# A fused trunk block: the first gain row spread by TensorE, indexer heads one projection later, and norm chains in a fixed queue order

## The chip, the cores and the metric

One Trainium2 chip, one core. The metric is the device time of one execution in microseconds (us); lower is better. The profile is one more execution, taken by the hardware profiler. In its rows PE is TensorE, PEld its weight loads, DVE is VectorE, ACT is ScalarE, POOL is GpSimd and SP is SyncE; a trailing q (SPq, POOLq) is that engine's own queue issuing a DMA.

## The reference, cut to what matters

```
def rms_norm(x, g):
    return x * rsqrt(mean(x*x) + 1e-6) * g

h = rms_norm(x, g_mix_pre)                      # x: 512 tokens x 1024
(lru_x, lru_gate, pool_in, q, k, v, q_idx, k_idx, w_idx, gates) = split(h @ w_in)
ya = rg_lru(conv(lru_x)) * gelu(lru_gate)       # recurrence branch
yb = multiscale_pool(pool_in)                   # pooling branch
score = sum_h w_idx[h] * relu(q_idx[h] @ k_idx) # 8 indexer heads, then top 128 keys
yc = attention(q, k, v over the chosen keys)    # sparse attention branch
merged = sum(sigmoid(gates) * (branch @ w_branch))
x = x + rms_norm(merged @ w_out, g_mix_post)
h = rms_norm(x, g_mem_pre)
x = x + rms_norm(cross_attention(h, mem) @ w_mem_o, g_mem_post)
h = rms_norm(x, g_ffn_pre)
x = x + rms_norm((silu(h @ w_gate) * (h @ w_up)) @ w_ffn_out, g_ffn_post)
```

All data are float32. The output is x, 512 x 1024.

## The kernel before, in words

**Precision.** Every float32 product is made of three TensorE products. An operand is split into a high part (ACT casts it, `A.copy`) and a low part (DVE or POOL subtracts, `V.tensor_sub`); `mm3` (lines 89 to 92) multiplies high by high, high by low and low by high into one PSUM bank. Each weight tile of 128 x 1024 is loaded by SP into one of six `raw` slots and split by `split_next` (lines 180 to 206). Activations with features on the partitions stand in `hh` and `hl`, 128 x 8 x 512.

**Order.** The program is traced by Python, and a planner then orders each engine's instructions by its own estimate of when they become ready; it takes what is earlier in the program first among those that are ready. Inside `tc.manual_schedule()` (the start, up to line 431) the traced order is kept. `tc.keep_in_program_order(ins)` keeps one instruction behind the one traced just before it on its engine; nothing else is held by it. All waits between engines are by semaphore, and each engine takes its own list strictly in order.

**Start.** SP loads the two halves of tokens 0 to 127, then the row `g_mix_pre` broadcast to all 128 partitions (512 KB written, `gain`, line 228), then tokens 128 to 255, two weight tiles, and the rest. TensorE multiplies the identity 15 times (`keep_warm`). For each of the four groups of 128 tokens: ACT squares and sums, `rstd` makes the root from a power on POOL and one Newton step on DVE, `start_norm` (line 317) multiplies by root and gain, `turn_pe` (line 294) transposes on TensorE, `turn_out` (lines 302 and 303) splits the result into `hh` and `hl`. The first products follow on tokens 0 to 255 (line 422).

**Indexer.** For each pair of heads m = 0 to 3 there is one projection (`unit`, 24 products of 512 columns). `stacked_queries` splits its result and sends it by four DMAs from SP into `QI`. `idx_heads(m)` makes six score products (line 451), each followed by a relu on ACT (line 459) and a multiply-add on DVE (lines 462 and 464). In the loop over m = 1 to 3, `idx_heads(m - 1)` follows the projection of pair m; `idx_heads(3)` follows the projection of keys and values. After it `value_task` transposes the values (line 516).

**Attention.** A written list of steps (line 797) sets in which tick each score (S), transposition (T) and value product (A) is traced.

**Norms between the sub-layers.** Class `Residual` holds one group of 128 tokens after a sub-layer: `scaled` (sum of squares on ACT, times gain on DVE, line 914), `scale` (root), `add` (to x, line 930), `square`, `scale2`, `norm` (line 939) and `turn` (transposition into `hh` and `hl`). After the cross attention's output projection, `project` calls `after_o(t)` when group t is complete. Groups 0 and 1 are turned within the projection. The FFN's first two column pairs (four weight tiles) are then multiplied for tokens 0 to 255; after the third tile stand `R[3].norm()` and the turn of group 2, after the fourth the turn of group 3. The tile products of tokens 256 to 511 follow.

**FFN.** From the third column pair on, a seven-product scheme (class `Pair`) works on sums of weight quarters and of token quarters. `token_sums` builds the token side; `first` to `fourth` build the weight side of the next pair while the current one is multiplied. `first` is line 1183's cast of a weight tile and line 1186's subtraction.

Of the kernel before, what the change touches and what calls it, by code (L numbers as in the profile page):

```python
# [9 lines left out]
F32 = mybir.dt.float32  # L10
F32R = mybir.dt.float32r
AF = mybir.ActivationFunctionType
OP = mybir.AluOpType
AX = mybir.AxisListType

P = 128
D = 1024
# [5 lines left out]
EPS = 1e-6  # L23
# [42 lines left out]
def hybrid_block_kernel(ctx: ExitStack, tc: tile.TileContext, a: dict, out: bass.AP):  # L66
    nc = tc.nc
    V, A, T, G, SP = nc.vector, nc.scalar, nc.tensor, nc.gpsimd, nc.sync

    base = ctx.enter_context(tc.tile_pool(name="base", bufs=1))  # L70
    psum = ctx.enter_context(tc.tile_pool(name="psum", bufs=1, space=bass.MemoryType.PSUM))
    PS = Slots(psum, "ps", 8, 512)
# [3 lines left out]
    GB = Slots(base, "gb", 2, 1024)  # L76
# [3 lines left out]
    T2 = Slots(base, "t2_", 10, 512)  # L80
# [5 lines left out]
    def f32(ap):  # L86
        return ap.bitcast(F32)
# [140 lines left out]
    def gain(name):  # L228
        g = GB.take([P, D])
        src = a[name]  # L230
        SP.dma_start(g, bass.AP(tensor=src.tensor, offset=src.offset, ap=[[0, P], [1, D]]))
        return g

    warm = base.tile([P, 1], F32, name="warm")
    V.memset(warm, 0.0)
    A.activation(warm, warm, AF.Tanh)
# [2 lines left out]
    V.memset(half, -0.5)  # L239
    for c in range(2):  # L240
        SP.dma_start(xs[0][:, 0, c * 512:(c + 1) * 512], x_in[0:P, c * 512:(c + 1) * 512])
    g_pre = gain("g_mix_pre")
    SP.dma_start(xs[0][:, 1], x_in[P:2 * P, :])
    load_ahead(2)
    SP.dma_start(xs[1][:, 0], x_in[2 * P:3 * P, :])
# [1 line left out]
    ident = base.tile([P, P], F32, name="ident")  # L247
# [8 lines left out]
    def keep_warm(n):  # L256

        ps = PS.take([P, P])
        for _ in range(n):
            T.matmul(ps, ident, ident, start=True, stop=True)  # L260
        PS.give(ps)

    start = tc.manual_schedule()
    start.__enter__()
    keep_warm(WARM[0])

    def rstd(parts):

        u, w, y, c = col(name="u"), col(name="w"), col(name="y"), col(name="c")
        if len(parts) > 1:  # L270
            V.tensor_scalar(u, parts[0], parts[1], EPS, op0=OP.add, op1=OP.add)  # L271
        else:
            V.tensor_scalar(u, parts[0], EPS, None, op0=OP.add)
        G.tensor_tensor(y, u, half, op=OP.pow)  # L274
        V.tensor_scalar(w, u, -0.5, None, op0=OP.mult)

        def finish():
            V.scalar_tensor_tensor(c, y, w, y, op0=OP.mult, op1=OP.mult)  # L278
            V.scalar_tensor_tensor(y, c, 1.5, y, op0=OP.add, op1=OP.mult)  # L279
            return y  # L280
        return finish

    def sum_sq(src, scratch):

        ss = col(name="ss")
        A.activation(scratch, src, AF.Square, scale=D ** -0.5, accum_out=ss)  # L286
        return ss

    def turn_pe(src):
# [8 lines left out]
    def turn_out(pss, hh, hl, t, last=True):  # L298
        dst = slice(t * P, (t + 1) * P)
        for q, ps in enumerate(pss):  # L300
            h = hh[:, 4 * q:4 * q + 4, dst]
            A.copy(h, ps)
            V.tensor_sub(hl[:, 4 * q:4 * q + 4, dst], ps, f32(h))  # L303
        if last:
            PS.give(*pss)

# [4 lines left out]
    hh, hl = HH.take([P, KD, S], F32R), HL.take([P, KD, S], F32R)  # L311
# [8 lines left out]
    ss = [sum_sq(*X0[1])]  # L320
# [4 lines left out]
    pss = turn_pe(X0[0][1])  # L325
# [5 lines left out]
    pss = turn_pe(X0[1][1])  # L331
# [6 lines left out]
    ss = [[sum_sq(*X0[t])] for t in range(2, 4)]  # L338
# [49 lines left out]
    def unit(o, w):  # L388
        unit_piece(o, w, 0, S)
        give_w(w)  # L390
# [90 lines left out]
    def idx_heads(m):  # L481
        for h in (2 * m, 2 * m + 1):
            for b in range(1, 4):
                idx_head(b, h)

    for m in range(1, 4):
        w = take_w()
        ps = PS.take([P, S])
        unit(ps, w)
        if m == 1:  # L490
            pw = PS.take([P, 4, 8])
            for t in range(4):
                T.transpose(pw[:, t], wf[64:72, t * P:(t + 1) * P], ident[64:72, 64:72])
            V.tensor_scalar(wq, pw, 8 ** -0.5, None, op0=OP.mult)
            PS.give(pw)
            T2.give(wf)
            vector_task()
            softplus_task()
        stacked_queries(ps, QI, m)
        PS.give(ps)  # L500
        idx_heads(m - 1)

    w = take_w()
    ps = PS.take([P, S])
# [3 lines left out]
    A.copy(vf[64:128], ps[64:128])  # L508
    PS.give(ps)

    idx_heads(3)

    def value_task():
# [16 lines left out]
    for i, name in enumerate(("lru_w_a", "lru_w_x")):  # L530
        t = T2.take([P, 4, P])
        G.memset(t, 0.0)
        src = a[name][0].rearrange("(m s) i j -> s i m j", s=2)
# [4 lines left out]
    t = T2.take([P, 4, P])  # L538
# [108 lines left out]
    for m in range(4):  # L647
        w = take_w()
        ps = PS.take([P, S])
# [5 lines left out]
    for g in GROUPS:  # L655
        w = take_w()
        ps = PS.take([P, S])
# [9 lines left out]
    for m in range(4):  # L667
        w = take_w()
        ps = PS.take([P, S])
# [123 lines left out]
    def steps_of(text):  # L793
# [1 line left out]
        return [(lambda s=s: kind[s[0]](int(s[1]), int(s[2]))) for s in text.split()]  # L795

    ticks = collections.deque(steps_of(t) for t in (
# [3 lines left out]

# [8 lines left out]
    for m in range(4):  # L810
        w = take_w()
        ps = PS.take([P, S])
# [58 lines left out]
    X = [xs[t // 2][:, t % 2] for t in range(4)]  # L871
# [36 lines left out]
    def scaled(pss, g, dst, scratch):  # L908

        ss = []  # L910
        for c in range(2):
            cs = slice(c * 512, (c + 1) * 512)
            ss.append(sum_sq(pss[c], scratch[:, cs]))
            V.tensor_mul(dst[:, cs], pss[c], g[:, cs])
        PS.give(*pss)
        return ss

    class Residual:
# [8 lines left out]
            self.f = rstd(self.ss)  # L927

        def add(self):
            V.scalar_tensor_tensor(X[self.t], self.b8[:, 0], self.f(), X[self.t], op0=OP.mult, op1=OP.add)  # L930

        def square(self):
            self.ss = [sum_sq(X[self.t], self.b8[:, 0])]
# [2 lines left out]
            self.f = rstd(self.ss)  # L936

        def norm(self):
            V.scalar_tensor_tensor(self.b8[:, 1], X[self.t], self.f(), self.g2, op0=OP.mult, op1=OP.mult)  # L939

        def turn(self, more=None):
            pss = turn_pe(self.b8[:, 1])
# [7 lines left out]
    hh, hl = HH.take([P, KD, S], F32R), HL.take([P, KD, S], F32R)  # L950
    R = []
# [20 lines left out]
    for m in range(4):  # L972
        w = take_w()
        ps = PS.take([P, NM])
# [19 lines left out]
    for i in range(4):  # L994
        w = take_w()
        for kk in range(2):
            k = 2 * i + kk
            for t in range(2):
                r = slice(t * P, (t + 1) * P)
# [63 lines left out]
    for h in range(4):  # L1063
        w = take_w()
        ps = PS.take([P, S])
# [21 lines left out]
    hh, hl = HH.take([P, KD, S], F32R), HL.take([P, KD, S], F32R)  # L1087
    R = []

    def after_o(t, pss):  # L1090
        R.append(Residual(t, pss, g_post, g_next))
        R[t].scale()
        R[t].add()
        R[t].square()
        R[t].scale2()
        if t < 3:
            R[t].norm()


    whole = K8.take([P, 2, 4, 256])  # L1100
# [14 lines left out]
    def last_heads():  # L1115
# [3 lines left out]
    project(lambda k: om[0][:, k], lambda k: om[1][:, k], 4, 4, after_o, [  # L1119
        (0, 0), lambda: mem_av(2), lambda: mem_tr(3), (0, 1), (0, 2), last_heads, (1, 0), (0, 3),  # L1120
        (1, 1), (1, 2), (1, 3), (2, 0), (2, 1), (2, 2), (2, 3), (3, 0), (3, 1), lambda: R[0].turn(turn_tokens),
        (3, 2), (3, 3), lambda: R[1].turn(turn_tokens)])
    K8.give(*om)


# [31 lines left out]
    def token_sums(t, c12, d1, d3):  # L1157

        r = slice((t - 2) * P, (t - 1) * P)
        d2, d4 = T2.take([P, 4, P]), T2.take([P, 4, P])  # L1160
        V.scalar_tensor_tensor(d2, d3, -1.0, whole[:, 0, :, r], op0=OP.mult, op1=OP.subtract)
        V.scalar_tensor_tensor(d4, d2, -1.0, whole[:, 1, :, r], op0=OP.mult, op1=OP.subtract)
        for name, src in (("t2", d2), ("t1", d1), ("t3", d3), ("t4", d4)):
            if name not in tokens:
                tile_ = K8.take([P, 2, 4, TH], F32R)
                tokens[name] = (tile_[:, 0], tile_[:, 1], tile_)
            h, l = (x[:, :, r] for x in tokens[name][:2])
            tc.keep_in_program_order(A.copy(h, src))
            tc.keep_in_program_order(V.tensor_sub(l, src, f32(h)))
        T2.give(c12, d1, d2, d3, d4)  # L1170
# [99 lines left out]
    pss = [PS.take([P, S]) for _ in range(NFIRST)]  # L1270
    for c in range(2):
        for i in range(NFIRST):
            unit_piece(pss[i], ws[i], c * 256, c * 256 + 256)
            if c == 0 and i == 2:
                R[3].norm()
                ds = R[2].turn(turn_tokens)
        if c == 0:
            token_sums(3, *R[3].turn(turn_tokens))
            token_sums(2, *ds)
            K8.give(whole)  # L1280
            tokens.update(b11=quad(0, 0), b21=quad(1, 0), b22=quad(1, 1))
            scratch = K8.take([P, 2, KD, P])
            cur = Pair(NFIRST // 2)
            for f in (cur.first, cur.sums, cur.second, cur.third, cur.fourth):
                f(f in (cur.first, cur.sums))
# [7 lines left out]
    old = None  # L1293
    while cur is not None:
        nxt = Pair(cur.m + 1) if cur.m + 1 < NFF else None
        if nxt is None:
            state["last"] = len(specs)
        cur.p1()
        if nxt:
            nxt.sums()  # L1300
        if old:
            old.p3()
        cur.p2()
        if old:
            old.p4()
        if nxt:
            nxt.first()
        cur.p6()
        if nxt:
            nxt.second()  # L1310
        cur.p5()
        cur.p7()
        if nxt:
            nxt.third()
            nxt.fourth()
        old, cur = cur, nxt
# [75 lines left out]
```

## Time and profile before

| | us |
|---|---|
| median of 3 runs | 889.28 (888.46 to 889.8) |
| the profiled execution | 890.12 |
| its span, first to last instruction | 888.3 |
| TensorE busy in the span | 867.3 (98%) |
| VectorE busy | 606.6 (68%) |
| ScalarE busy | 399.0 (45%) |
| GpSimd busy | 200.6 (23%) |

The profiled execution lies 0.84 us above the median of the runs. A busy share is the time in which an engine had an instruction running; a stretch in which TensorE has none is a wait, and the profile names what ended it. PEclk is the share of full clock that TensorE was granted: 1.00 is 2.4 GHz, 0.50 is 1.2 GHz.

### The profile page before, as it was taken

Reading aid. Unit: us, or ns where it says so; the run is one execution under the profiler, and the core shown is the slowest. Engines: PE = TensorE matmul, PEld = TensorE weight load, DVE = VectorE, ACT = ScalarE, POOL = GpSimd, SP = SyncE. Lnnn points to the kernel's source line nnn. Section 1 sums busy time; section 2 is a strip of 40 time slices with the busy share of each in tenths; the row PEclk is TensorE's granted clock in tenths of the full one; section 3 lists DMA queues with packets and bytes.
Section 4 is the critical chain, followed back from the end, with each engine's and each line's share of the span. In section 5 each row is a group of like instructions: output and inputs, shape, how many; then the busy total and the mean of one; then the engine's idle time right before and its main releaser. Section 6 shows DMA issues by size and latency. Waiting matters only on the chain. (4 is left out here: it accounts for less than half of the span.)

```text
span 888.3 us, 12970 instructions
## 1 busy us (share of the span) xinstructions
PE 867.3 (98%) x4923; PEld 754.6 (85%) x4923; DVE 606.6 (68%) x1089; ACT 399.0 (45%) x669; POOL 200.6 (23%) x195
## 2 busy tenths in 40 slices
PE   7999999999999999999999998999999999999996
PEld 7788888888878888888888878999999999888885
DVE  5859989973775656442696778987888878732225
ACT  4555644223654544331565554554554455522121
POOL 2223267454344423210110011111111110000000
PEclk8999999999999999999999999999999999999999
DMA  8953227333333237333265302677777775433102
GB/s 252 240 129 99 80 63 200 94 95 95 83 86 86 68 86 261 106 105 96 82 187 159 95 1 48 151 157 171 163 154 152 166 172 135 126 95 95 47 1 95
DMA packets 128570, 106.02 MB, mean 119 GB/s; under 512 B 6208, under 2 KB 112252, under 8 KB 128508
## 3 DMA queue, kind: packets, MB, share of 16 engines
q1 hardware_dynamic: 120172, 90.52, 36.0%
q0 software_dynamic: 5760, 10.49, 7.5%
q10 hardware_dynamic: 2576, 4.19, 1.4%
q8 instruction: 38, 0.62, 0.3%
q14 instruction: 24, 0.20, 0.1%
HBM read 86.83 MB, written 2.10 MB: 100 GB/s over the span
## 5 line engine op out<-in xcount | busy, mean ns | idle before, releaser
L191 ACT CAST wh<-raw 128x1024 fp32r<-128x1024 f32 (+1 forms) x104 | 108.6, 1047 | 228.3 <-PE ps L91 108.2
L90 PE MATMUL ps<-hh,wh 128*128 128x512 f32 (+2 forms) x584 | 207.2, 355 | 0.0
L91 PE MATMUL ps<-hl,wh 128*128 128x512 f32 (+2 forms) x584 | 206.3, 353 | 0.4 <-DVE hl L303 0.4
L92 PE MATMUL ps<-hh,wl 128*128 128x512 f32 (+2 forms) x584 | 206.3, 353 | 0.0
L195 DVE TENSOR_TENSOR wl<-raw,wh 128x1024 fp32r<-128x1024 f32 x60 | 73.8, 1235 | 102.7 <-ACT wh L191 102.7
L91 PEld LDWEIGHTS ps<-hl,wh 128*128 128x128 f32 (+1 forms) x584 | 109.3, 187 | 16.0 <-DVE hl L303 0.6
L90 PEld LDWEIGHTS ps<-hh,wh 128*128 128x128 f32 (+1 forms) x584 | 109.4, 187 | 15.9 <-ACT t L459 0.2
L92 PEld LDWEIGHTS ps<-hh,wl 128*128 128x128 f32 (+1 forms) x584 | 109.2, 187 | 15.9
L90 PE MATMUL ps<-k,wh 128*128 128x256 f32 (+1 forms) x368 | 114.6, 311 | 0.0
L92 PE MATMUL ps<-k,wl 128*128 128x256 f32 (+1 forms) x368 | 114.3, 310 | 0.0
L91 PE MATMUL ps<-k,wh 128*128 128x256 f32 (+1 forms) x336 | 105.3, 313 | 0.0
L198 POOL TENSOR_TENSOR wl<-raw,wh 128x512 fp32r<-128x512 f32 (+1 forms) x44 | 59.2, 1346 | 153.9 <-ACT wh L191 139.7
L274 POOL TENSOR_TENSOR y<-u,half 128x1 f32<-128x1 f32 x26 | 16.4, 631 | 304.8 <-DVE u L271 259.3
L92 PE MATMUL ps<-wh,k 128*128 128x512 f32 x192 | 75.8, 395 | 0.0
L92 PEld LDWEIGHTS ps<-k,wl 128*128 128x128 f32 x368 | 69.4, 188 | 4.3
L90 PEld LDWEIGHTS ps<-k,wh 128*128 128x128 f32 x368 | 69.3, 188 | 4.1
L91 PE MATMUL ps<-wl,k 128*128 128x512 f32 x176 | 69.4, 394 | 0.5 <-DVE wl L195 0.5
L1186 DVE TENSOR_TENSOR wl<-raw,wh 128x1024 fp32r<-128x1024 f32 x40 | 49.0, 1225 | 30.4 <-ACT wh L1183 30.1
L90 PE MATMUL ps<-wh,k 128*128 128x512 f32 x176 | 69.0, 394 | 0.0
L1183 ACT CAST wh<-raw 128x1024 fp32r<-128x1024 f32 x40 | 42.0, 1051 | 59.2 <-PE ps L91 52.9
L91 PEld LDWEIGHTS ps<-k,wh 128*128 128x128 f32 x336 | 63.3, 188 | 4.2
L199 POOL TENSOR_TENSOR wl<-raw,wh 128x512 fp32r<-128x512 f32 (+1 forms) x44 | 61.5, 1397 | 0.0
(250 smaller groups left out, 1697.7 us busy)
## 6 DMA issues: line engine op xcount, KB each, us to landing
raw<-in_w_in SPq DMA_DIRECT2D x45, 512.0 KB, 3.9
raw<-in_w_ffn_in SPq DMA_DIRECT2D x44, 512.0 KB, 4.8
raw<-in_w_ffn_out SPq DMA_DIRECT2D x22, 512.0 KB, 3.6
raw<-in_w_branch SPq DMA_DIRECT2D x12, 512.0 KB, 3.4
raw<-raw POOLq DMA_DIRECT2D x20, 256.0 KB, 3.7
raw<-k POOLq DMA_DIRECT2D x20, 256.0 KB, 3.3
k<-t SPq DMA_DIRECT2D x32, 128.0 KB, 2.4
raw<-in_w_out SPq DMA_DIRECT2D x8, 512.0 KB, 3.4
```

The lines of the kernel that those rows point to most:

```text
L90: T.matmul(o, lh, rh, start=start, stop=False, skip_group_check=True)
L91: T.matmul(o, lh, rl, start=False, stop=False, skip_group_check=True)
L92: T.matmul(o, ll, rh, start=False, stop=stop, skip_group_check=True)
L191: copy = A.copy(h, src)
L195: V.tensor_sub(l, src, f32(h))
L198: G.tensor_sub(l[:, :c], src[:, :c], f32(h[:, :c]))
L199: G.tensor_sub(l[:, c:], src[:, c:], f32(h[:, c:]))
L274: G.tensor_tensor(y, u, half, op=OP.pow)
L1183: copy = A.copy(h, src)
L1186: V.tensor_sub(l, src, f32(h))
```

## The change

Four edits. The gain row of the first norm is loaded once (4 KB, from ACT's queue, ahead of everything else there), turned on TensorE to a column and spread to all partitions by eight transpositions of broadcast columns, copied to SBUF by DVE; this stands ahead of `keep_warm`. The indexer heads of a pair follow one projection later. One tick of the attention list traces its scores ahead of its transposition. The chains of `Residual` after the cross attention are kept in traced order on ACT and DVE, with a new order for groups 0 and 1; the norm of group 3 moves into its chain; the turn of group 1 moves ahead of the projection's last block; the turns of groups 2 and 3 and the first cast of the fourth column pair are kept in order too.

```
+    grow = T2.take([8, P])
+    A.dma_start(grow, a["g_mix_pre"][0].rearrange("(k p) -> k p", p=P))
...
-    g_pre = gain("g_mix_pre")
...
     start = tc.manual_schedule()
     start.__enter__()
+    g_pre = GB.take([P, D])
+    gcol = base.tile([P, 8], F32, name="gcol")
+    ps = PS.take([P, 8])
+    T.transpose(ps, grow, ident[:8, :8])
+    V.tensor_copy(gcol, ps)
...
+    for q in range(2):
+        ps = PS.take([P, 4, P])
+        for k in range(4):
+            T.transpose(ps[:, k], gcol[:, 4 * q + k:4 * q + k + 1].to_broadcast([P, P]), ident)
+        V.tensor_copy(g_pre[:, q * 512:(q + 1) * 512], ps.rearrange("p k c -> p (k c)"))
+        PS.give(ps)
     keep_warm(WARM[0])
+    pins = {"on": False}
+    def queued(ins):
+        if pins["on"]:
+            tc.keep_in_program_order(ins)
...
-        idx_heads(m - 1)
+        if m > 1:
+            idx_heads(m - 2)
...
+    idx_heads(2)
     idx_heads(3)
...
-        "S00 S01", "S02 S03", "S10 S11", "T00 S12 S13",
+        "S00 S01", "S02 S03", "S10 S11", "S12 S13 T00",
...
     def after_o(t, pss):
+        pins["on"] = True
         R.append(Residual(t, pss, g_post, g_next))
+        if t == 1:
+            R[0].square()
         R[t].scale()
         R[t].add()
-        R[t].square()
-        R[t].scale2()
-        if t < 3:
-            R[t].norm()
+        for r in R[-2:] if t == 1 else R[t:] if t else ():
+            if r is not R[0]:
+                r.square()
+            r.scale2()
+            r.norm()
+        pins["on"] = False
...
-        (3, 2), (3, 3), lambda: R[1].turn(turn_tokens)])
+        (3, 2), lambda: R[1].turn(turn_tokens), (3, 3)])
...
             if c == 0 and i == 2:
-                R[3].norm()
+                pins["on"] = True
                 ds = R[2].turn(turn_tokens)
+                pins["on"] = False
         if c == 0:
-            token_sums(3, *R[3].turn(turn_tokens))
+            pins["on"] = True
+            ds3 = R[3].turn(turn_tokens)
+            pins["on"] = False
+            token_sums(3, *ds3)
...
-            nxt.first()
+            nxt.first(old is None)
```

The calls wrapped in `queued` are those of `rstd` on DVE, `sum_sq`, `turn_out`, the multiplication in `scaled`, `add` and `norm`.

## Rows read from the trace of the kernel before

**Rows 1.** The page's first part: busy us (share of span) xinstructions.

```profile
PE 867.3 (98%) x4923; PEld 754.6 (85%) x4923; DVE 606.6 (68%) x1089; ACT 399.0 (45%) x669; POOL 200.6 (23%) x195
```

**Rows 2.** Waits of TensorE, whole span: us in total, times, longest us.

```profile
PE ps L294 <- DVE k L317: 3.2, 2, 1.7
PE ps L294 <- DVE k L939: 3.1, 1, 3.1
PE ps L294 <- ACT wh L1183: 1.7, 1, 1.7
PE ps L451 <- DMA k<-t: 1.7, 1, 1.7
...
PE ps L516 <- ACT t L508: 0.7, 1, 0.7
PE ps L761 <- DVE t L751: 0.7, 1, 0.7
```

**Rows 3.** Timeline of the start, all engines: start us, us, instruction [idle before <-releaser].

```profile
1.42 6.12 PE L260 MATMUL ps<-ident 128*128 128x128 f32 x30 [1.42 <-POOL ident masks.py:199]
...
3.84 0.63 ACT L286 ACTIVATE k<-k 128x512 f32<-128x512 f32 x1 [1.60 <-DMA k<-in_x]
...
6.34 0.16 DVE L279 SCALAR_TENSOR_TENSOR y<-c,y 128x1 f32<-128x1 f32 x1
8.43 1.42 DVE L317 SCALAR_TENSOR_TENSOR k<-k,y,gb 128x512 f32<-128x512 f32 x2 [1.92 <-DMA gb<-in_g_mix_pre]
...
9.23 1.61 PE L294 MATMUL ps<-ident,k 128*128 128x128 f32 x8 [1.69 <-DVE k L317]
...
9.80 1.06 ACT L286 ACTIVATE k<-k 128x1024 f32<-128x1024 f32 x1 [4.63 <-DMA k<-in_x]
...
15.88 0.56 PE L90 MATMUL ps<-hh,wh 128*72 128x256 f32 x1
```

**Rows 4.** Windows of the start, PE alone: stretch, PE busy, PEclk, DMA share, GB/s.

```profile
10.00:17.00 7.00, 5.52 (x25) 0.51 1.07 318
```

**Rows 5.** Timeline of the indexer's heads: PE, then DVE.

```profile
39.28 1.29 PE L451 MATMUL ps<-ik,k 128*128 128x256 f32 x6 [1.68 <-DMA k<-t]
...
48.56 4.35 DVE L464 SCALAR_TENSOR_TENSOR sc<-t,wq,sc 128x256 f32<-128x256 f32 x6
```

**Rows 6.** Windows, all engines: PE, PEld, DVE, ACT, POOL busy (x), PEclk, DMA share, GB/s.

```profile
80.00:100.00 20.00, 20.00 (x89) 16.23 (x88) 20.00 (x41) 12.34 (x18) 2.54 (x3) 1.00 0.30 80
...
600.00:650.00 50.00, 50.00 (x426) 50.00 (x425) 41.14 (x62) 25.26 (x35) 8.66 (x10) 1.00 0.72 159
```

**Rows 7.** Timeline of the way from cross attention into the FFN: DVE and PE.

```profile
518.76 1.28 DVE L939 SCALAR_TENSOR_TENSOR k<-k,y,gb 128x1024 f32<-128x1024 f32 x1
...
526.12 1.28 DVE L939 SCALAR_TENSOR_TENSOR k<-k,y,gb 128x1024 f32<-128x1024 f32 x1
...
527.54 1.07 PE L294 MATMUL ps<-ident,k 128*128 128x128 f32 x8 [1.73 <-ACT wh L1183]
528.04 0.68 DVE L303 TENSOR_TENSOR hl<-ps,hh 128x512 fp32r<-128x512 f32 x1
...
535.00 1.28 DVE L939 SCALAR_TENSOR_TENSOR k<-k,y,gb 128x1024 f32<-128x1024 f32 x1
...
544.90 1.27 DVE L939 SCALAR_TENSOR_TENSOR k<-k,y,gb 128x1024 f32<-128x1024 f32 x1
...
546.32 1.94 PE L294 MATMUL ps<-ident,k 128*128 128x128 f32 x8 [3.09 <-DVE k L939]
...
561.17 1.22 DVE L1186 TENSOR_TENSOR wl<-k,wh 128x1024 fp32r<-128x1024 f32 x1
...
562.95 0.28 PE L90 MATMUL ps<-k,wh 128*128 128x256 f32 x1
```

**Rows 8.** Windows of the same way, PE alone: stretch, PE busy, PEclk, DMA share, GB/s.

```profile
528.50:532.50 4.00, 3.57 (x16) 0.57 0.02 4
546.00:550.00 4.00, 3.68 (x19) 0.57 0.18 33
```

More of the change, by code (lines that the diff above doesn't have):

```diff
@@ L264, in hybrid_block_kernel @@
     start.__enter__()
+    g_pre = GB.take([P, D])
[4 more added lines that the diff above has]
+    PS.give(ps)
+    T2.give(grow)
+    for q in range(2):
[3 more added lines that the diff above has]
+        V.tensor_copy(g_pre[:, q * 512:(q + 1) * 512], ps.rearrange("p k c -> p (k c)"))
+        PS.give(ps)
     keep_warm(WARM[0])
+    pins = {"on": False}
+    def queued(ins):
+        if pins["on"]:
+            tc.keep_in_program_order(ins)
     def rstd(parts):
@@ L270, in rstd @@
         if len(parts) > 1:
-            V.tensor_scalar(u, parts[0], parts[1], EPS, op0=OP.add, op1=OP.add)
+            queued(V.tensor_scalar(u, parts[0], parts[1], EPS, op0=OP.add, op1=OP.add))
         else:
-            V.tensor_scalar(u, parts[0], EPS, None, op0=OP.add)
+            queued(V.tensor_scalar(u, parts[0], EPS, None, op0=OP.add))
         G.tensor_tensor(y, u, half, op=OP.pow)
-        V.tensor_scalar(w, u, -0.5, None, op0=OP.mult)
+        queued(V.tensor_scalar(w, u, -0.5, None, op0=OP.mult))
         def finish():
-            V.scalar_tensor_tensor(c, y, w, y, op0=OP.mult, op1=OP.mult)
-            V.scalar_tensor_tensor(y, c, 1.5, y, op0=OP.add, op1=OP.mult)
+            queued(V.scalar_tensor_tensor(c, y, w, y, op0=OP.mult, op1=OP.mult))
+            queued(V.scalar_tensor_tensor(y, c, 1.5, y, op0=OP.add, op1=OP.mult))
             return y
@@ L285, in sum_sq @@
         ss = col(name="ss")
-        A.activation(scratch, src, AF.Square, scale=D ** -0.5, accum_out=ss)
+        queued(A.activation(scratch, src, AF.Square, scale=D ** -0.5, accum_out=ss))
         return ss
@@ L301, in turn_out @@
             h = hh[:, 4 * q:4 * q + 4, dst]
-            A.copy(h, ps)
-            V.tensor_sub(hl[:, 4 * q:4 * q + 4, dst], ps, f32(h))
+            queued(A.copy(h, ps))
+            queued(V.tensor_sub(hl[:, 4 * q:4 * q + 4, dst], ps, f32(h)))
         if last:
@@ L913, in scaled @@
             ss.append(sum_sq(pss[c], scratch[:, cs]))
-            V.tensor_mul(dst[:, cs], pss[c], g[:, cs])
+            queued(V.tensor_mul(dst[:, cs], pss[c], g[:, cs]))
         PS.give(*pss)
@@ L929, in add @@
         def add(self):
-            V.scalar_tensor_tensor(X[self.t], self.b8[:, 0], self.f(), X[self.t], op0=OP.mult, op1=OP.add)
+            queued(V.scalar_tensor_tensor(X[self.t], self.b8[:, 0], self.f(), X[self.t], op0=OP.mult, op1=OP.add))
         def square(self):
@@ L938, in norm @@
         def norm(self):
-            V.scalar_tensor_tensor(self.b8[:, 1], X[self.t], self.f(), self.g2, op0=OP.mult, op1=OP.mult)
+            queued(V.scalar_tensor_tensor(self.b8[:, 1], X[self.t], self.f(), self.g2, op0=OP.mult, op1=OP.mult))
         def turn(self, more=None):
```

## The prediction, made before any run of the changed kernel

> **What bounds the kernel now.** I read the page first, then TensorE's waits, then the stretches in which they lie. The reader is to see that TensorE has something running for 867.3 of 888.3 us [rows 1]: nothing the other engines do counts unless it ends a wait of TensorE or its low clock. So the change can win at most what TensorE loses now, place by place. The list of its waits [rows 2] has six entries that this change can touch: 3.2 us (two waits) for the first norm, 3.1 and 1.7 us on the way into the FFN, 1.7 us for the first indexer heads, 0.7 us for the values' transposition and 0.7 us for an attention transposition: 11.1 us in all. The windows add the clock: from 10 to 17 us TensorE was granted 0.51 [rows 4], and on the way into the FFN 0.57 in two stretches of 4 us [rows 8], each after one of those waits. Half clock loses half of the time it lasts: a grant of 0.57 over 4 us costs 1.7 us, less the 0.2 us or so that fall on idle time, so about 1.5 us each time.
>
> **The start.** Removed: a 512 KB load. Root and Newton step of the first 128 tokens are done at 6.34 + 0.16 = 6.50, but the multiplication starts at 8.43, released by the gain's load [rows 3]: 1.9 us is the most that an early gain can give to this chain. Without those 512 KB tokens 128 to 255, whose square waits for its load until 9.80, also come earlier: at the 318 GB/s of the stretch from 10 to 17 us [rows 4] that load is worth 1.6 us, so they no longer bind.
>
> Added: a 4 KB load on ACT's queue, one transposition, a small copy, eight transpositions, two copies of 512 columns, all ahead of `keep_warm` on TensorE and of the first root on DVE. No row shows so small a load on an empty machine. Its nearest row is the first half of the tokens, issued at the same time and used at 3.84; it can't need longer than that unless it queues behind it. I take 3.4, bounds 2.5 and 4.5. A transposition is 1.61 / 8 = 0.20 us, a 512-column subtraction out of PSUM 0.68 [rows 3, 7]. So: 3.4 + 0.2 + 0.2 (small copy, by the 0.16 of a small DVE operation) + 4 x 0.20 + 0.68 + 0.68 = 6.0, the second four transpositions beside the first copy. DVE begins the first root only then; of the time from 3.84 to 6.50 it is what two squares of 0.63 leave, 1.4 us, less their readouts, so 1.3; thus the multiplication starts at 7.3 instead of 8.43: 1.1 us sooner, between 0.1 and 1.9.
>
> Moved: `keep_warm`'s 15 products start when the transpositions end, at 5.2 instead of 1.42. They took 6.12 us [rows 3]. If they take as long, TensorE reaches the first group's transpositions at 11.3, later than 9.23; if the late ones run at the rate of the FFN (50 us / 426 = 0.117 us for 256 columns [rows 6]) it gets there at about 9.3. From there follow eight transpositions, two `keep_warm` products, eight transpositions, two products. In the good case that is 9.3 + 1.0 + 0.5 + 1.3 + 0.5 = 12.6, and the low parts from DVE are complete about 13.4, where the first product starts; before it starts at 15.88 and has half clock until 17 [rows 3, 4]. Bad case: 11.3 + 1.6 + 1.1 + 2.1 + 1.1 = 17.2. I take 2.0 us won, bounds 3.0 won and 1.3 lost.
>
> The row shows the first transpositions 7.8 us into a machine that had been multiplying since 1.42, and still a low grant right behind the 1.69 us wait [rows 3, 4]. The Trainium skill ("TensorE: Matmul & The Clock Gate", Part 1, The HAM clock gate) says that the throttled state is the default and that activity releases it. That speaks against this edit: TensorE now sits idle until the 4 KB have landed, so it would be released later. By it the start would be the bad case; the trace agrees as far as the clock's fall behind a wait goes.
>
> **Indexer heads.** Nothing is added; six score products and their relus and multiply-adds move behind the next projection, four times; the last two sets of six stand together. The first score products waited 1.68 us for the DMAs of their queries [rows 5]; behind another projection (24 x 20 / 89 = 5.4 us [rows 6]) these have landed. The values' transposition waited 0.74 us for a copy on ACT; now twelve head products stand in between. Won: 2.4 us, of which I take 2.2; bounds 0 (the wait moves to PSUM or to weights) and 2.4. What it costs: six multiply-adds of 4.35 / 6 = 0.73 us at most [rows 5] leave a stretch in which DVE had room and join one where it has none (20.00 of 20 us busy from 80 to 100 [rows 6]). Up to 4.4 us of DVE work comes later in front of the top-k rounds. TensorE runs without a wait there, so most of it is covered; I take 0.8 us lost, bounds 0 and 3.3.
>
> **The attention tick.** T00 waited 0.7 us [rows 2] for probabilities; two sets of scores now stand in front. Won 0.6, bounds 0 and 0.7.
>
> **The way into the FFN.** Today each group's chain (gain, root, add, square, root, norm) is interleaved with whatever else is ready. `norm` starts at 518.76, 526.12, 535.00 and 544.90 [rows 7]: 7.4, 8.9 and 9.9 us apart, ever slower, since subtractions of turned groups and of FFN weights slip in. TensorE waits for the second (1.73 us, put down to an ACT cast that stood in front) and the fourth (3.09 us).
>
> By the new order group 1's two multiplications, root and add come before group 0's second root. So group 0's norm ends later, at about 522.0 instead of 520.0 (two 0.68, one 1.28, less gaps), and group 1's at 524.6 instead of 527.4, as POOL's power and ACT's square of one group run beside DVE's work of the other. TensorE ended its projection at 527.54 - 1.73 = 525.81. Now the turn of group 1 (1.04 us) lies inside it, with waits of about 0.2 and 0.5 us for the two norms: 527.5. The first FFN tile needs the low parts of both turned groups, four subtractions of 0.68 us, and these have no pin: they fit in the gaps of group 2's pinned chain, the last needed one at about 528.5. So 1.0 us of wait. Four tiles of 24 products (96 x 0.117 = 11.3 us) and the turn of group 2 (0.9) later, TensorE is at group 3's turn at 540.7. The norm of group 3: the chain of group 2 takes 9.7 us from 524.6 (8.9 before, and four subtractions in it) and that of group 3, half overlapped, 5.2 more: 539.5. So the turn starts at 540.7 instead of 546.32, 5.6 us sooner, and if TensorE has no long wait the low clock behind 546 goes too: 1.5 us. Together 7.1.
>
> What is late next is DVE's path from this turn to the third pair's second weight split. Before, it was busy without a gap from the turn to 561.17 + 1.22 = 562.39, and TensorE needed it at 562.95 [rows 7]: 0.56 us of slack. The cast of the fourth pair, which sat early in the chain (the 1.73 us wait names it), is now pinned behind the first product of the third, so its 1.22 us subtraction joins that path. I charge 0.6. Net 6.5; bounds 9.0 (all waits and both low clocks gone) and 2.3 (below).
>
> **Sum.** 2.0 + 2.2 - 0.8 + 0.6 + 6.5 = 10.5 us. The profiled execution took 890.12, so 879.6; the median of the runs shown is 0.84 lower, so 878.8.
>
> **Rivals.** (a) The wait moves in the FFN's entry. The four unpinned subtractions go behind group 2's pinned chain instead of into its gaps: add and square and second root, some 3 us, stand in front, and TensorE waits 3 us more at the first tile, long enough to lose 1.5 us of clock there, and again at the turn. For it: the multiplications of group 2 did go ahead of ready work before. Against it: the wait for POOL's power leaves gaps that a planner fills. It leaves 2.3 us here and 884 in all (878.8 + 4.2 = 883.0, 884 with some of (b)).
> (b) The start loses: low clock until `keep_warm` is over at 11.3, since TensorE idles before the 4 KB land; first product at 17.2. For it: the fall of the clock behind the 1.69 us wait. Against it: once the row is there TensorE is busy without a break. 2.0 + 1.3 = 3.3 us less won: 882.1. The Trainium skill's page named above is on the side of this case.
> (c) Slower. The deferred multiply-adds make DVE late through the whole saturated stretch, and TensorE meets it three times, at the recurrence, pooling and query projections: three waits of 3.3 us with 1.6 us of low clock behind each is 14.7 us, against 11.3 won: 892.7. It decides once the waits for DVE between 66 and 250 us exceed 11.3 us. Against it: no such wait stands in the list today.
> (d) Nothing changes: the planner already placed these instructions nearly so, and the waits only change their names: 889.3.
>
> **How the numbers follow.** Forecast 0.60, (a) 0.16, (b) 0.10, (c) 0.08, (d) 0.06. A measurement of this kernel can tell about 0.2%, 1.8 us, from no change; forecast, (a) and (b) are all faster by more: 0.86. Same 0.06, slower 0.08. The range: low end all upper bounds, 3.0 + 2.4 + 0.7 + 9.0 = 15.1 off 889.28, is 874.2, and 873.5 with clock won elsewhere; high end (a) with (b), 883.0 + 3.3 = 886.3. Cases (c) and (d), 0.14, lie outside.
>
> **What would show it.** Right: the multiplication of the first norm at about 7.3 us and the first real product before 14; no wait for the queries' DMA near 39 us; four norms in the FFN's entry about 2 to 3 us apart for the first pair, the last done before TensorE needs it; PEclk 1.00 from the first FFN tile on. Wrong: `keep_warm` running past 11 us; the first FFN tile waiting for DVE's low parts; new waits for DVE between 66 and 250 us.

## The result, and the profile of the changed kernel

The changed kernel takes 883.94 us (median of five runs, 883.01 to 885.71), the kernel before 889.80 on the same chip: ratio 0.9936, 95% interval 0.992 to 0.9952. It is faster by 5.9 us where 10.5 were forecast; the time lies inside the range. The profiled execution took 883.94 us with a span of 882.0. One run of the seventh experiment, 1214.89 us long at a mean granted clock of 0.655, is left out of all medians and ratios below.

The page's first part, busy us (share of span) xinstructions, against [rows 1]:

```profile
PE 863.5 (98%) x4932; PEld 749.8 (85%) x4932; DVE 608.9 (69%) x1092; ACT 399.2 (45%) x669; POOL 202.1 (23%) x195
```

TensorE's waits over the whole span, us in total, times, longest, against [rows 2]:

```profile
PE ps L270 <- DMA t<-in_g_mix_pre: 3.1, 1, 3.1
PE ps L91 <- DVE hl L325: 2.9, 4, 1.0
PE ps L90 <- ACT t L1274: 2.5, 1, 2.5
PE ps L91 <- DVE t L416: 1.0, 2, 0.6
PE ps L90 <- ACT hh L324: 0.7, 2, 0.5
...
PE ps L316 <- ACT hh L324: 0.3, 1, 0.3
PE ps L90 <- ACT t L415: 0.2, 1, 0.2
```

All six waits of [rows 2] are gone. Three new ones matter: the copy of line 1274 (2.5 us), low parts behind the turns of the FFN's entry (line 325), and lines 415 and 416 in the stretch where VectorE is full (1.2 us together).

Where each part was won or lost is read by setting the start of the n-th of the 4,500 products of lines 90 to 92 in the one trace against the start of the n-th in the other; the difference is called the lead here, and its places are given in times of the kernel before. The changed kernel is ahead by 3.1 us at the fifth product, 5.7 behind the indexer heads (66 us), 3.6 behind the waits of lines 415 and 416 (129 us), 3.5 at 200, 4.1 at 319, 4.0 at 521, 8.9 from 549 to 563, and 6.0 from 566 us to the end.

**Start**, all engines, start us, us, instruction [idle before <-releaser], against [rows 3]:

```profile
3.10 0.24 PE L270 MATMUL ps<-ident,t 8*128 8x8 f32 x1 [3.10 <-DMA t<-in_g_mix_pre]
...
3.60 1.97 PE L277 MATMUL ps<-ident,gcol 128*128 128x128 f32 x8 [0.26 <-DVE gcol L271]
...
5.36 4.09 PE L261 MATMUL ps<-ident 128*128 128x128 f32 x30
...
7.54 1.41 DVE L339 SCALAR_TENSOR_TENSOR k<-k,y,gb 128x512 f32<-128x512 f32 x2
...
9.29 1.04 PE L316 MATMUL ps<-ident,k 128*128 128x128 f32 x8
...
12.46 0.36 PE L90 MATMUL ps<-hh,wh 128*72 128x256 f32 x1
...
13.39 0.34 PE L91 MATMUL ps<-hl,wh 128*72 128x256 f32 x1 [0.57 <-DVE hl L325]
```

Windows of TensorE there: stretch, busy (instructions), PEclk, DMA share, GB/s.

```profile
4.00:6.00 2.00, 2.00 (x12) 1.00 1.04 345
...
8.00:10.00 2.00, 2.00 (x20) 1.00 1.04 379
10.00:17.00 7.00, 6.17 (x51) 1.00 1.18 307
```

The multiplication starts at 7.54 (forecast 7.3), `keep_warm` ends by 9.45 (forecast 9.3 in the good case), the first product starts at 12.46 instead of 15.88; the second waits for its low parts until 13.39. From 10 to 17 us the grant is 1.00 where it was 0.51 [rows 4].

**Way into the FFN and what follows**, all engines, against [rows 7]:

```profile
516.70 1.28 DVE L963 SCALAR_TENSOR_TENSOR k<-k,y,gb 128x1024 f32<-128x1024 f32 x1
...
519.16 1.28 DVE L963 SCALAR_TENSOR_TENSOR k<-k,y,gb 128x1024 f32<-128x1024 f32 x1
...
523.38 1.29 DVE L954 SCALAR_TENSOR_TENSOR k<-k,y,k 128x1024 f32<-128x1024 f32 x1
523.52 0.38 PE L90 MATMUL ps<-hh,k 128*128 128x256 f32 x1 [0.46 <-ACT hh L324]
...
524.58 1.28 DVE L325 TENSOR_TENSOR hl<-ps,hh 128x512 fp32r<-128x512 f32 x2
...
525.32 0.39 PE L91 MATMUL ps<-hl,k 128*128 128x256 f32 x1 [0.92 <-DVE hl L325]
...
527.21 1.28 DVE L963 SCALAR_TENSOR_TENSOR k<-k,y,gb 128x1024 f32<-128x1024 f32 x1
...
534.69 1.28 DVE L963 SCALAR_TENSOR_TENSOR k<-k,y,gb 128x1024 f32<-128x1024 f32 x1
...
537.19 1.03 PE L316 MATMUL ps<-ident,k 128*128 128x128 f32 x8
...
538.46 0.39 PE L90 MATMUL ps<-hh,k 128*128 128x256 f32 x1 [0.24 <-ACT hh L324]
...
540.23 0.39 PE L91 MATMUL ps<-hl,k 128*128 128x256 f32 x1 [1.02 <-DVE hl L325]
...
552.85 0.87 POOL L1244 DMA_DIRECT2D raw<-k  x1 [0.32 <-issue]
...
558.22 0.62 ACT L1212 CAST t<-raw 128x512 fp32r<-128x512 f32 x1 [2.13 <-DMA raw<-k]
558.74 1.04 ACT L1212 CAST wh<-k 128x1024 fp32r<-128x1024 f32 x1
...
559.68 0.36 ACT L1274 COPY t<-ps 128x256 f32<-128x256 f32 x1
...
560.10 0.39 PE L90 MATMUL ps<-x,wh 128*128 128x256 f32 x1 [2.48 <-ACT t L1274]
```

The turn of group 3 starts at 537.19 without a wait, 9.1 us before its old place and 5.1 more than the lead of 4.0 that TensorE brought along. In the two stretches that had low clock the grant is 1.00, against [rows 8]:

```profile
528.50:532.50 4.00, 4.00 (x36) 1.00 0.39 122
546.00:550.00 4.00, 4.00 (x36) 1.00 0.00 0
```

But at 560.10 product 7 of the third pair waits 2.48 us. It writes the PSUM bank that the copy of product 6 (line 1274) must have read. That copy had nothing to wait for but its place: on ScalarE's list it stands behind two casts, and the first of them waited until 558.22 for the transfer that POOL issued at 552.85.

### The profile page after: what moved, and what is told of

It is laid out like the page before. It is cut to its first block, busy times and chain, and to the rows that moved or that the text cites. A ratio compares the mean times of both kernels' runs of the same rounds, so it can differ in the third digit from the quotient of the medians.

```text
span 882.0 us, 12995 instructions
## 1 busy us (share of the span) xinstructions
PE 863.5 (98%) x4932; PEld 749.8 (85%) x4932; DVE 608.9 (69%) x1092; ACT 399.2 (45%) x669; POOL 202.1 (23%) x195
## 4 chain that ended last, share of the span: by engine, by line
PE 81%; DVE 12%; POOL 2%; issue 2%; ACT 1%; DMA 1%; ACTq 0%; DVEq 0%; POOLq 0%
PE ps L91 25%; PE ps L92 25%; PE ps L90 25%; PE ps L473 2%; DVE k L938 1%; PE ps L800 1%; DVE k L954 1%; POOL t L632 1%; DVE hl L325 1%; DVE t L577 1%; DVE work L496 1%; DVE wl L195 1%; DVE m L495 1%; DVE k L963 1%; POOL y L296 1%
```

## The experiments

Two theories of the 2.48 us. **A**: the pin on the next pair's first cast (`nxt.first(old is None)`) makes weight work late. **B**: the pin only shifts places; the time is lost by a transfer that lands late, and by a copy that stands behind the cast of what it brings. Ratios are to the kernel before on the same chip, with the 95% interval.

**1. The cast free again.**

```
-            nxt.first(old is None)
+            nxt.first()
```

> The changed kernel with one edit taken back: the first cast of the fourth column pair is not held in order. Theory A (holding it back is what makes the product at 560.10 wait 2.48 us, since it pushes the weight work of the third pair's successors together): the wait goes, about 2.5 us won, 881.5. Theory B (the wait comes from one late share of the accumulating DMA that landed at 558.19, 15 of 16 shares being there at 556.52, and from the cast that waits for it in front of the copy on ScalarE's list; holding the first cast is innocent): the cast goes back into the norm chains ahead of the FFN, the wait near 560 stays between 0.8 and 2.5 us, and the time is 883.9 within 1 us either way.

881.70 us, ratio 0.99 (0.9884 to 0.9915): about the time that A gave, and below the changed kernel. In its trace nothing waits near 560. But TensorE also came there 2.2 us later than in the changed kernel: the waits behind group 3's turn were 0.49 and 1.15 instead of 0.24 and 1.02, and a stretch of 0.66 followed. And ScalarE's list is another one: both casts of `wh<-k` run at 555.09, and the late cast, at 558.11, hardly waits, since the list comes to it only when the transfer has landed (last share at 558.09). That the pin costs something in the changed kernel is shown; by which way is not.

**2. The instruction fetch moved.** Two of the query projections are multiplied in halves:

```
+        for c in range(2) if h in (1, 2) else ():
+            for k in range(KD):
+                cs = slice(c * 256, c * 256 + 256)
+                mm3(ps[:, cs], w[0][:, k], w[1][:, k], hh[:, k, cs], hl[:, k, cs], k == 0, k == KD - 1)
...
```

> The changed kernel with two projections of the cross attention's queries multiplied in two halves of 256 columns instead of one of 512: the same columns in 48 more products, which moves TensorE's instruction fetches in the FFN some 5 to 6 us earlier against its work, away from the accumulating DMA of 552.85. Theory B (late share behind the fetch packet): the DMA's last share lands with the others, the wait at 560 falls from 2.48 to at most 0.8 us, 1.7 to 2.4 us won, about 882. Theory A: the wait stays, 883.9 (or a little more, should the halves cost something).

883.35 us, ratio 0.9921 (0.9907 to 0.9934). DMA queues and issues (packets, MB, share; KB each, median us to landing) of the changed kernel from 552.5 to 558.5, then of this one from 552.8 to 557.5:

```profile
q8 instruction: 1, 0.02, 1.5%
...
raw<-k POOLq DMA_DIRECT2D x2, 256.0 KB, 4.9
```

```profile
q0 software_dynamic: 288, 0.52, 65.7%
...
raw<-k POOLq DMA_DIRECT2D x2, 256.0 KB, 4.1
```

In the changed kernel one packet of instructions (16 KB, 1.5% of 16 engines over 6 us, which is 1.4 us of one engine) runs amid the transfer. The transfer comes in sixteen shares, each with a landing of its own: fifteen were there at 556.52, the last at 558.19. With the fetch elsewhere the cast starts at 556.78, 3.7 us after the issue at 553.11 instead of 5.4, and the wait at product 7 falls to 0.78 us. That part of B is shown, and against the changed kernel's trace 1.7 us are won there, as expected. The median is lower by 0.6 us only. In this trace 0.4 us go at the halved projections, 0.5 at the FFN's entry, where the clock fell (0.66 from 525 to 530 us, below), and 0.5 behind the wait. The clock isn't the whole of it: two of the five runs have a mean grant of 0.999 and took 883.2 and 883.4 all the same. Where the rest goes in those is open.

**3 and 5. The late cast behind the copy.** In the third experiment the fourth cast was only traced behind product 6; in the fifth it is also held there:

```
-            for f in (cur.first, cur.sums, cur.second, cur.third, cur.fourth):
+            for f in (cur.first, cur.sums, cur.second, cur.third):
...
         cur.p6()
+        if old is None:
+            cur.fourth(True)
```

> The changed kernel with the fourth of the second pair's weight casts traced behind the copy of product 6 in the first turn of the FFN's loop, so that on ScalarE the copy need not stand behind the cast that waits for the DMA. If the in-order list of ScalarE carries the delay (theory B), the wait of product 7 at 560.10 goes or falls under 0.8 us and about 2 us are won, 882, unless the cast is then late for its own product. Theory A: the wait is of the work and not of the order, 883.9 to 884.5.

885.42 us, ratio 0.9944 (0.9931 to 0.9957). By itself it tells nothing of the theories: the planner put the cast in front of the copy again, and product 7 waited 2.15 us. But its program differs from the fifth's by the hold alone, so it is what the fifth is to be set against. ScalarE in the third:

```profile
558.65 0.62 ACT L1212 CAST t<-raw 128x512 fp32r<-128x512 f32 x1 [1.72 <-DMA raw<-k]
559.18 1.04 ACT L1212 CAST wh<-k 128x1024 fp32r<-128x1024 f32 x1
560.12 0.36 ACT L1274 COPY t<-ps 128x256 f32<-128x256 f32 x1
```

> The edit of the third experiment, made effective: in the FFN's first turn the fourth weight cast of the second pair is traced behind the copy of product 6 and held there on ScalarE's list (in the third experiment the planner had put it in front again). Theory B (ScalarE's list carries the delay of the late transfer to TensorE): the copy runs as soon as product 6 ends, near 557.9, the wait of 2.48 us falls under 0.8 us, 1.5 to 2 us won against the changed kernel, about 882. Theory A (the held first cast makes the weight work late, wherever the copy stands): a wait for weights of 1.5 us or more takes the place of the wait for the copy, 883.5 to 884.5.

882.15 us, ratio 0.9901 (0.9884 to 0.9917); profiled 882.09 against 883.94 (changed kernel) and 885.89 (third). ScalarE in the fifth:

```profile
556.68 1.05 ACT L1212 CAST wh<-k 128x1024 fp32r<-128x1024 f32 x1
557.63 0.36 ACT L1274 COPY t<-ps 128x256 f32<-128x256 f32 x1
558.80 0.62 ACT L1212 CAST t<-raw 128x512 fp32r<-128x512 f32 x1 [0.81 <-DMA raw<-k]
```

The transfer lands as late as before (5.2 us after its issue, 5.3 in the changed kernel), the cast waits for it as before, and TensorE doesn't: no wait at product 7, and the lead behind 566 us is 8.1 instead of 6.0 (4.1 in the third, where the clock also fell behind the wait). The pin is still there. ScalarE's list is the cause.

**12. The pin taken away with the copy free** (the first edit, put on the kernel of the ninth experiment, below, which has the fifth's).

> The kernel of the ninth experiment (held fourth cast, heads mixed; 880.85) with the first cast of the fourth column pair free again, as in the first experiment. If holding it was harmful only because the copy of product 6 stood behind what it displaced (theory B), nothing is left to win once the copy is free: 880.9, or 0.5 to 1.5 us slower, as the cast and its subtraction go back into the norm chain. If holding it costs by itself (theory A), 1 us or more is won: under 880.

880.74 us, ratio 0.989 (0.9875 to 0.9904), against 880.85 and 0.9898 (0.9884 to 0.9911) with the pin. Once the copy is free, the pin costs nothing that can be told. A falls as a cause of its own. So what the first experiment won it won at the copy, by its other list or by coming there later; which of the two is not shown.

**4. The norm chains alone** (the kernel before, with the edits of `Residual`, `after_o`, the turns and their pins, and the pin on the first cast).

> The kernel before with the norm chains' edits alone (order of the chains, turn of group 1 earlier, everything held in order there); start, indexer heads and attention tick as before. The changed kernel's trace puts 4.9 us won between 522 and 549 and 2.8 lost near 560. If the loss hangs on the instruction fetch's place (theory B), the fetches keep their place of the kernel before plus what the earlier turns shift, and the loss may be absent: 4.9 won, 884.9, or with the loss 887.5. Theory A: the loss is part of this edit, 887.5.

886.36 us, ratio 0.9952 (0.9938 to 0.9966). In its trace the lead is 4.75 us from 549 to 563 and 3.3 at the end: a wait of 0.93 us at the same product, and the rest of the loss before and behind it. So the chains alone bring between 3.3 us (profiled execution against profiled execution) and 4.1 (the medians); the loss near 560 is smaller with the same pin, and TensorE gets there 4.1 us later. The transfer's last share is 0.14 us behind the others here, not 1.67. That fits B but doesn't by itself rule A out.

**6, 10 and 11. The remaining waits of the FFN's entry.** All three have the fifth's edit. In the sixth the turn of group 3 moves into the fourth tile, with group 2's token differences behind it (the rest of the edit is left out):

```
+            early = c == 0 and i == 3
+            unit_piece(pss[i], ws[i], c * 256, c * 256 + 256, range(5) if early else range(KD))
...
+            if early:
+                unit_piece(pss[i], ws[i], c * 256, c * 256 + 256, range(5, KD))
```

> The edit before, and the turn of group 3 put into the fourth FFN tile behind its fifth of eight blocks, with the token differences of group 2 held behind the splitting of group 3. The changed kernel waits 0.24 and 1.02 us behind this turn; three blocks (1.05 us) now stand there. About 1.0 us less than the kernel with the held cast alone, near 881. Rival: VectorE is the bound there (norm ends at 535.97, then 1.28 us for group 2's low parts and two unpinned additions), the wait moves and nothing is won, 882.

882.52 us, ratio 0.9902 (0.9884 to 0.992): no gain over the fifth by the medians. The two waits behind this turn are gone, but in the profiled execution the clock fell behind the first tile. Windows of TensorE, from 525 to 530 us, in this kernel and in the fifth:

```profile
525.00:530.00 5.00, 4.70 (x26) 0.66 0.00 0
```

```profile
525.00:530.00 5.00, 4.69 (x39) 1.00 0.00 0
```

The waits ahead of this stretch are the same (0.46 and 0.91 here, 0.46 and 0.92 there). Three of the four runs, at a mean grant of 0.996, took 882.5 to 882.8 us; the one at 0.999 took 880.77, near the 881 that was expected. One run doesn't show the gain, but the edit isn't refuted either.

In the tenth the chains of groups 2 and 3 are interleaved as those of 0 and 1, in `after_o` (part of the edit):

```
+        if t == 3:
+            R[2].scale2()
+            R[3].scale()
+            R[2].norm()
+            R[3].add()
...
```

with `R[2].add()` and `R[2].square()` behind the turn of group 1, and the token copies of groups 0 and 1 behind both their splittings.

> The kernel with the held cast, and groups 2 and 3 interleaved as 0 and 1 are: the splitting of turned groups 0 and 1 goes ahead of the copies of their tokens on ScalarE and ahead of group 2's addition on VectorE, and group 3's multiplications go into the gap of group 2's second square. The waits of 0.46 and 0.92 us at the first FFN tile fall to about 0.4 together, and group 3's norm ends no later than before: 1.0 us won, and more in executions that lose clock behind these waits; 881. Rival: VectorE's path into the third pair sets the end of this stretch, the 1.0 us comes back as a wait near 560: 882.2.

884.44 us, ratio 0.9941 (0.9927 to 0.9954): a miss. The first tile's wait shrank to 0.62, but the expectation that group 3's norm would end no later was wrong:

```profile
538.79 1.07 PE L316 MATMUL ps<-ident,k 128*128 128x128 f32 x8 [2.14 <-DVE k L963]
```

> Both edits before together, and the turn of group 3 inside the fourth tile (the sixth experiment). If each takes away waits that nothing else hides: 0.8 + 1.0 + 1.0 us less than with the held cast alone, near 879.5. If VectorE's path into the third pair is the bound, the last two come back as waits behind 555: 881.3.

881.39 us, ratio 0.9904 (0.9891 to 0.9918). The same wait of 2.14 us stands in it; nothing is won over the ninth (below) alone.

**7 and 9. The indexer heads.** First, in the changed kernel, the heads back where they were; then, in the fifth's kernel, only pair 2's set taken out of the two that stand together at the end (shown here):

```
         if m > 1:
             idx_heads(m - 2)
+        if m == 3:
+            idx_heads(2)
...
-    idx_heads(2)
     idx_heads(3)
```

> The changed kernel with the indexer heads where they were. The waits of 1.68 and 0.74 us return: 2.4 us lost. If the new waits for VectorE and ScalarE between 66 and 128 us (1.9 us against the kernel before) come from the later multiply-adds, they go and the net is 0.5 us slower, 884.5. If they come from the earlier start or the tick instead, they stay, 886.3.

886.09 us (median of four), ratio 0.995 (0.9932 to 0.9968). Its waits of TensorE between 30 and 135 us:

```profile
PE ps L473 <- DMA k<-t: 1.1, 1, 1.1
PE ps L538 <- ACT t L530: 0.7, 1, 0.7
```

and those of the changed kernel from 100 to 126 us, which this one has not:

```profile
104.63 0.50 PE L91 MATMUL ps<-t,k 128*128 128x512 f32 x1 [0.48 <-DVE t L416]
123.62 0.51 PE L90 MATMUL ps<-t,k 128*128 128x512 f32 x1 [0.18 <-ACT t L415]
124.68 0.50 PE L91 MATMUL ps<-t,k 128*128 128x512 f32 x1 [0.56 <-DVE t L416]
```

The lead stays at 3.7 to 3.8 us from 40 to 128 us and is 4.3 at 319, against 4.1 with the later heads. At 66 us the changed kernel is 1.9 us ahead of this one (5.7 against 3.7), about the sum of this one's two waits, and at 319 us 0.2 behind. So the heads' edit won 1.9 us against this run and gave all of it back, by VectorE's lateness: the new waits come from the later heads, as the expectation's first case had it, but the net of 0.5 us isn't there. The total is longer than the 884.5 of that case; its trace shows stretches of 0.66 and 0.67 near 525 and 560, so the lead at 319 us prices the edit and the total doesn't.

> The kernel with the held cast (882.15) and another place for one set of heads: pair 2 already behind the projection of pair 3, so that only the last set stands behind the projection of keys and values. The first wait (1.68 us, for the queries' transfer) stays away. If the loss of 1.9 us behind 66 us comes from two sets of multiply-adds standing together at the end, most of it goes, less up to 0.7 us for the values' transposition that has only one set in front again: 0.5 to 1.2 us won, 881.2. If the loss comes from the first set's delay, nothing is won: 882.2 to 882.9.

880.85 us, ratio 0.9898 (0.9884 to 0.9911), the fastest here together with the twelfth. One wait is left between 30 and 135 us:

```profile
PE ps L541 <- ACT t L533: 0.3, 1, 0.3
```

and the lead at 319 us is 5.1, 1.0 more than with two sets together, although the start won 0.5 us less in this trace (2.6 against 3.1). From 66 to 200 us the lead falls by 0.1 us (4.6 to 4.5), where it fell by 2.2 in the changed kernel.

**8. The gain row alone** (on the kernel before).

> The kernel before with the gain row's edit alone. The trace of the changed kernel has the first product 3.1 us earlier: 3.1 us won if all of it is kept to the end, 886.7 against 889.8, with the heads' waits as before. Rival: some of it is given back, at the queries' DMA near 39 us or at the FFN's entry, where the chain of norms sets the time: 1 to 2 us won, 888.

887.58 us, ratio 0.9981 (0.9965 to 0.9997). The lead is 3.2 us from the start to 522 us and 2.5 at the end. Nothing is given back at the queries' transfer, where TensorE waits 1.8 us as before; 0.7 us go at the FFN's entry. Nine of the twelve runs took 887.0 to 888.7 us; the other three, at a mean grant of 0.991, took 890.6 to 891.5.

## Why the prediction was right, and where it was too high

**The sum, term by term** (won, forecast against the changed kernel's trace): start 2.0, measured 3.1; heads 2.2, measured 2.5; VectorE's lateness 0.8 lost, measured 2.1; tick 0.6, measured 0.5; the way into the FFN 6.5 net, measured 2.0. That is 10.5 against 6.0, and the spans differ by 6.3.

**Start.** The good case held, and rival (b) didn't. The row of 4 KB was there at 3.10 (taken: 3.4). TensorE does run at half pace first, although the profile's PEclk reads 1.00: 12 instructions from 4 to 6 us against 20 from 8 to 10. Its instructions start 0.21 us apart until 6.6 us and 0.11 apart from 6.7 on, in time for `keep_warm` to end by 9.45. In the kernel before, where TensorE began 1.7 us sooner, the pace changed at 6.8. The Trainium skill ("TensorE: Matmul & The Clock Gate", Part 1, The HAM clock gate) has the throttled state as the default; by the pace the trace agrees with that. What rival (b) made of it, a low clock until 11.3, came in no trace: in the eleven other kernels with this start the pace changed between 7.0 and 9.1 us, and the lead at the fifth product is 2.5 to 3.7 us. The 1.1 us more than forecast are a choice: 2.0 was taken between a good case of up to 3.0 and a bad one, and the good case came. It also ended where it was forecast to end, with the low parts there at 13.39 (forecast about 13.4). The first product, which needs high parts alone, started before that, at 12.46, and the second then waited 0.57 us.

**Heads and tick.** Both mechanisms held. The tick's 0.5 us appear between 200 and 319 us, and not in the fourth and eighth experiment, which lack it. The cover was mis-sized: "most of it is covered; I take 0.8 us lost" measured 2.1, inside the bounds of 0 to 3.3. It is rival (c)'s mechanism at a small price: three waits of 0.2 to 0.6 us, no low clock behind them. They show 1.2 us of idle time, and the lead falls by 2.1 at them: the trace has a product of 512 columns run for 0.4 to 0.5 us while the next usually starts 0.23 behind it, so a wait costs time before it shows as idle. Seventh and ninth experiment show that the loss comes from the late sets, and that it goes when two of them no longer stand together at the end.

**The way into the FFN, up to 549 us.** 7.1 us were forecast, 4.9 came. The turn of group 3 came 5.1 us sooner than TensorE's lead explains (forecast 5.6), and both low clocks went. The norms of groups 0, 1 and 3 end at 517.98, 520.44 and 535.97; with the lead of 4.0 that is 522.0, 524.4 and 540.0, where 522.0, 524.6 and 539.5 were forecast. The first tile waited 0.46 and 0.92 us (forecast 1.0). Not in the sum were 0.24 and 1.02 us behind the turn of group 3, where TensorE now stands at the splitting that follows.

**"What is late next".** This is the step that failed: "I charge 0.6" for VectorE's path into the third pair. 2.9 us were lost (from 8.9 to 6.0), and on another engine. The path that I followed had its weights ready in time; what came late was the copy of product 6, on ScalarE, behind a cast that waits for a transfer. In the kernel before the same transfer landed 3.4 us after its issue (560.66 to 564.06), and the copy behind the cast, at 564.92, was early enough. The fifth experiment gives 2.1 us back by moving that one cast. The 0.8 that it still loses there (8.9 to 8.1) are about what was charged; a wait of 0.21 us for a weight cast at 555.13 is in it.

**Rivals.** (a) fell as a mechanism, though its time, 884, is the one that was measured. Two of the four subtractions ran in the gap of group 2's first root (521.68 and 522.34), the other two behind its addition (524.58) but ahead of its second root, and the first tile waited 0.46 and 0.92 us, without a fall of the clock in this execution, where (a) had 3 us more than the forecast. (d) fell with the time. Of the three signs of being wrong two appeared in small: the first tile waited for low parts, and there are new waits for VectorE between 66 and 250 us (1.0 us in all).

**Luck.** That the time lies in the range is partly luck. The range reached up to 886.3 for the sake of (a) and (b), and a wait that no case had took up that room; and the start and the heads won 1.4 us more than forecast, which hides part of what VectorE's lateness and the FFN lost. That both low clocks went holds for the profiled execution: two of the five runs, at mean grants of 0.995 and 0.997 instead of 0.999, took 885.7 us; where the clock fell in them is not recorded.

**What stays open.** Why the clock falls behind the first tile in some executions and not in others; so single traces of the FFN's entry differ by up to 2 us, and the medians of the kernels between 880.7 and 882.5 can't be ordered finely. Why the second experiment's total hardly moved is open too.

## What to carry to other kernels

When a change brings an engine forward, look at each list that it then catches up with, not only at the one that was busiest: the copy that frees a PSUM bank is short, but on an in-order list it is as late as the transfer that the cast before it waits for. Put such a copy ahead of a cast that waits for a DMA, and hold it there: here the order of tracing alone left the cast in front, and only the hold moved it (third and fifth experiment). Work that is deferred to cover one wait should be spread: the same heads with one set less at the end covered the same waits but for 0.3 us, and cost 0.1 us behind them instead of 2.2.

## What was not expected of the hardware

The fetch of TensorE's instructions is a transfer among the others: one packet of 16 KB, about 1.4 us of one DMA engine, delayed one share of sixteen by 1.7 us, and with it the whole transfer. In the eight traces in which such a packet ran amid this transfer (the changed kernel, the first, third, fifth and seventh to tenth experiment) it took 0.9 to 1.7 us, and the last share landed 0.9 to 1.8 us behind the fifteenth; in the second and eleventh, where none ran, 0.01 us behind. Its place moved with the number of TensorE's instructions: 48 more products in another layer took it from 555.2 to 547.5 us.

The same two waits (0.46 or 0.47 us, and 0.91 or 0.92) were followed by a grant of 0.66 over 5 us in the second, sixth and seventh experiment and by 1.00 in the changed kernel, the first, third, fifth, ninth and twelfth; those behind the turn of group 3 by 0.66 in the first (0.49 and 1.15 us) and by 1.00 in the twelfth (0.50 and 1.16). The wait at product 7 was followed by 1.00 in the changed kernel (2.48 us), and by 0.66 and 0.67 in the third and seventh experiment (2.15 and 2.34). The rise at the start varies as well: the pace changed at 6.7 us in the changed kernel and at 9.1 in the tenth experiment, which has the same start. The Trainium skill ("TensorE: Matmul & The Clock Gate", Part 1, The HAM clock gate) says that the same kernel gets its clock at different points from run to run; these rows agree, and show the same of the fall.
